# Half A's last mixer: from where its steps take their PSUM banks

## The chip, the core and the metric

The kernel runs on one core of one Trainium2 chip. The metric is the device time of one execution in microseconds, as the median of several runs. Shown beside it is one execution that the hardware profiler recorded, with its own time and the span from its first to its last instruction. The engines are TensorE (PE, matmuls and transposes; PEld is its loading of stationary operands), VectorE (DVE), ScalarE (ACT), GpSimd (POOL) and SyncE (SP), which issues most of the DMAs.

## The reference, cut to what matters

The program is one inference step of a two-layer encoder trunk over 1024 prompt frames and 64 frames of a running stream, width 1024, in fp32. Layer 0 mixes time with two linear recurrences, layer 1 with attention over bands of chunks. Each layer then has a SwiGLU channel mixer, and a layer norm follows each mixing:

```python
def swiglu(x, w_in, w_out):
    gate, up = jnp.split(x @ w_in, 2, axis=-1)
    return (jax.nn.silu(gate) * up) @ w_out
...
for layer in range(DEPTH):
    mix = ...   # layer 1: chunk_band_attention(x, ...), which ends with "@ w_o"
    x = layer_norm(DEEPNORM_ALPHA * x + mix, P['ln1_w'][layer], P['ln1_b'][layer])
    x = layer_norm(DEEPNORM_ALPHA * x + swiglu(x, P['ffn_w_in'][layer], P['ffn_w_out'][layer]),
                   P['ln2_w'][layer], P['ln2_b'][layer])
```

The attention has 16 heads of 64. A frame reads its own chunk of 64 frames and the 8 chunks before it, with a learned bias, a softmax, and the product with the values.

## The kernel before

**Halves.** The 1088 frames are worked on in two halves: half A (index 0) holds the first 384 prompt frames and the 64 stream frames, 448 columns; half B (index 1) holds the other 640 prompt frames. Each fp32 operand is split into a high and a low part (hi, lo), and a product is three matmuls: hi by hi, lo by hi, hi by lo. `gemm_ws` (lines 115 to 125, weights stationary) and `gemm_ts` (lines 127 to 137, frames stationary) issue them; their output tiles are all called gps. These are the dense products below.

**The mixer.** `ffn` (from line 915) is a generator that yields after each of 22 steps. A step loads two weight tiles of 512 KB (`load_w`, line 97 on SP, cast on line 100 on ACT, remainder on lines 105 on DVE and 107 on POOL), makes 2 x 24 matmuls of 448 columns for half A, and evacuates them on lines 927 to 940. After steps 3, 7, 11, 15, 17 and 21 the output group of `tsg` follows: its products with w_out go into the accumulators acc on lines 823 to 827. `load_w` has two raw buffers (wr) and four for each part (wh, wl); a mixer holds five hidden tiles (HB).

**The attention.** `attention(hf, hp, ...)` does two heads (a block, hp 0 to 7). It loads vt, ks, qs and bias on SP, then for each tile of 128 queries: scores (lines 1279 and 1280) into the PSUM tile sps, the sum with the bias and the maximum on DVE (1283), the exponential on ACT (1288), the division on POOL (1290), transposes into tp (1295), and the split into ph and pl (1305, 1306). For each group of tiles follow the products with the values (1321) into op and the evacuation, lines 1325 (ACT) and 1326 (DVE). A half-B block has four such groups, so its fourth line 1326 is its end. Its output goes to DRAM (og_d, line 1330, issued by ACT).

**PSUM.** There are eight banks. The pool gp has three from the start. The attention's pool atps has five: one sps of two banks and three of the tag t. When atps is closed, the pool gp2 may take these five. `bank()` gives out the tiles of the dense products, by a counter:

```python
self.bcount += 1
if self.gp2 and self.bcount % 8 > 2:
    return self.gp2.tile([128, 512], F32, tag="g2", name="gps", bufs=5)
return self.gp.tile([128, 512], F32, tag="g", name="gps", bufs=3)
```

Three numbers of eight fall to gp and five to gp2, once gp2 is there; the counter runs on either way.

**The order around the change.** Layer 1 of half B's attention is written as a loop over the blocks 2 to 7 with two steps of half A's last mixer behind each, steps 0 to 11 (blocks 0 and 1 come earlier, between half B's q and k products). Behind the loop the mixer's steps go on. At step `JM` = 16 the text turns to half B: it loads the attention's output from og_d into xh and xl (`load_xt`, lines 213 to 215, issued behind step 16's last weight load), loads the residual into acc, and runs `proj` with w_o (k-tiles 4 to 7 first, then 0 to 3), with the mixer's steps 17 to 20 between its tiles. xh and xl lie where ph and pl of the last blocks were. After that half B's last mixer, `s_ffn`, ends the kernel.

The text's order isn't the order on the engines. The framework makes every engine's queue when the program is built, going by the text's order and taking a later piece where an earlier one isn't ready; a tile of a pool that was opened in the place of another waits for the release of what lay there.

Of the kernel before, what the change touches and what calls it, by code (L numbers as in the profile page):

```python
# [14 lines left out]
PS = bass.MemoryType.PSUM  # L15
# [67 lines left out]
class Kern:  # L83
# [1249 lines left out]
    def run(self):  # L1333
        nc, tc, a = self.nc, self.tc, self.a
# [133 lines left out]
                for _ in range(2):  # L1468
                    next(f)
        es_at.close()  # L1470
        self.gp2 = self.ctx.enter_context(tc.tile_pool(name="gp2", bufs=1, space=PS))
        self.tpsum = self.bank
        for j in f:
            if j == self.JM:
                accp = self.ctx.enter_context(tc.tile_pool(name="accB1", bufs=1, side="right"))
                self.xt[1] = self.xt_tiles(xbp, 1)
                with tc.tile_pool(name="yr2", bufs=1, side="right") as yp, tc.issue_after(self.last_w):
                    self.load_xt(1, self.og_d, (4, 5, 6, 7, 0, 1, 2, 3), pool=yp)
                    self.paired = True
                    acc1 = self.load_acc(1, self.x_d, accp)  # L1480
                xs, sums = self.s_operands(self.ctx.enter_context(tc.tile_pool(name="sx", bufs=1, side="right")),
                                           self.ctx.enter_context(tc.tile_pool(name="st", bufs=1, side="right")))
                self.proj(1, acc1, "w_o", self.layer_norm(1, acc1, "ln1", 1, sums=sums), between=lambda i: next(f) if i < 4 else None)
# [89 lines left out]
```

## Time and profile before

| | us |
|---|---|
| median of 3 runs | 3156.28 (3156.26 to 3160.05) |
| profiled execution | 3154.14 |
| its span, first to last instruction | 3152.4 |
| PE busy in it | 3036.0 |
| DVE, ACT, POOL busy | 2019.7, 1263.5, 1353.0 |
| DRAM moved by DMA | 395.10 MB |

Rows of the profile read as follows. A row of a table by stretches has the start and end of the stretch, its length, and for each engine the busy us with the count of instructions; then the mean clock that PE was granted (1.00 is full), the share of the DMA engines, and GB/s. A row in order of time has the start, the us, the engine, the line of the kernel, the operation, output <- input by the program's names, their size, the count of merged instructions, and in brackets the idle time before it and what ended that. SPq and ACTq are DMA issues on the queues of SP and ACT. Matmuls are pipelined, so the spacing of their starts, not the length of one, is what each costs.

### The profile page before, as it was taken

The numbers are of one execution on the slowest core, as the hardware profiler recorded it, in microseconds if no ns is written. First come the engines' busy times: TensorE is split into PE (matmuls) and PEld (weight loads), VectorE is DVE, ScalarE is ACT, GpSimd is POOL, SyncE is SP. The second block draws the span as 40 slices with busy tenths as digits, with TensorE's granted clock in tenths as the row PEclk, the third lists the DMA queues.
The fourth block names the chain that finished last, engine by engine and source line by source line (L and its number), as shares of the span: only waits on it lengthen the run. The fifth ranks groups of instructions, "written<-read, shape, count | busy, mean of one in ns | idle before, by whom it ended". The sixth has DMA issues, their size and how long they took to land.

```text
span 3152.4 us, 50043 instructions
## 1 busy us (share of the span) xinstructions
PE 3036.0 (96%) x17468; PEld 2695.1 (85%) x17468; DVE 2019.7 (64%) x4933; ACT 1263.5 (40%) x2753; POOL 1353.0 (43%) x1481
## 2 busy tenths in 40 slices
PE   8999998899999999999999999999998899899998
PEld 7888887788888878888899898999996788799987
DVE  5677885979898664465553645355565458866567
ACT  4454553335445324244342223354444323333332
POOL 2354433545454234343332323344454335754444
PEclk9989999789999999999999999999998899999999
DMA  6553444434434238434433224765454143322122
GB/s 204 139 158 112 111 123 112 145 99 121 134 104 111 87 127 281 138 115 121 117 114 98 82 92 155 227 185 163 139 147 117 63 150 98 113 94 94 62 86 74
DMA packets 297340, 395.10 MB, mean 125 GB/s; under 512 B 125376, under 2 KB 218424, under 8 KB 297088
## 3 DMA queue, kind: packets, MB, share of 16 engines
q1 hardware_dynamic: 295936, 389.28, 41.5%
q8 instruction: 138, 2.26, 0.3%
q10 hardware_dynamic: 1152, 2.62, 0.2%
q14 instruction: 114, 0.93, 0.1%
HBM read 319.44 MB, written 75.51 MB: 125 GB/s over the span
## 4 chain that ended last, share of the span: by engine, by line
PE 79%; DVE 9%; DMA 5%; POOL 3%; issue 3%; ACT 2%; SPq 0%; POOLq 0%; DVEq 0%; ACTq 0%
PE gps L123 11%; PE gps L124 11%; PE gps L125 11%; PE gps L134 8%; PE gps L135 7%; PE gps L137 7%; PE gps L1058 2%; PE gps L1059 2%; PE gps L1060 2%; PE op L1321 2%; PE tp L1295 2%; DVE t L548 1%; PE sps L1279 1%; DVE x L550 1%; PE ps L621 1%
## 5 line engine op out<-in xcount | busy, mean ns | idle before, releaser
L107 POOL TENSOR_TENSOR wl<-wr,wh 128x512 fp32r<-128x512 f32 (+2 forms) x289 | 509.3, 1766 | 680.7 <-ACT wh L100 634.2
L123 PE MATMUL gps<-xh,wh 128*128 128x320 f32 (+1 forms) x2188 | 749.6, 343 | 8.7 <-ACT xh L214 6.1
L124 PE MATMUL gps<-xl,wh 128*128 128x320 f32 (+1 forms) x2188 | 747.7, 342 | 0.6 <-DVE xl L215 0.6
L125 PE MATMUL gps<-xh,wl 128*128 128x320 f32 (+1 forms) x2188 | 745.1, 341 | 0.8 <-DVE wl L105 0.7
L100 ACT CAST wh<-wr 128x1024 fp32r<-128x1024 f32 x352 | 367.4, 1048 | 503.8 <-PE gps L124 166.4
L105 DVE TENSOR_TENSOR wl<-wr,wh 128x512 fp32r<-128x512 f32 (+2 forms) x289 | 286.0, 990 | 264.0 <-ACT wh L100 261.8
L123 PEld LDWEIGHTS gps<-xh,wh 128*128 128x128 f32 x2188 | 416.7, 191 | 30.5 <-ACT xh L214 6.1
L125 PEld LDWEIGHTS gps<-xh,wl 128*128 128x128 f32 x2188 | 415.9, 190 | 19.2 <-DVE wl L105 1.5
L124 PEld LDWEIGHTS gps<-xl,wh 128*128 128x128 f32 x2188 | 416.2, 190 | 18.4 <-DVE xl L215 1.0
L1290 POOL TENSOR_SCALAR s<-s,mx 128x640 f32<-128x640 f32 (+5 forms) x144 | 203.0, 1410 | 268.2 <-DVE mx L1289 234.5
L134 PE MATMUL gps<-wh,xh 128*128 128x512 f32 x661 | 261.5, 400 | 3.2 <-ACT xh L1088 2.5
L137 PE MATMUL gps<-wh,xl 128*128 128x512 f32 x661 | 259.1, 398 | 4.8 <-DVE xl L215 4.8
L135 PE MATMUL gps<-wl,xh 128*128 128x512 f32 x661 | 261.8, 398 | 0.9 <-DVE wl L105 0.9
L135 PE MATMUL gps<-wl,hh 128*128 128x512 f32 x572 | 226.4, 397 | 0.0
L134 PE MATMUL gps<-wh,hh 128*128 128x512 f32 x572 | 226.0, 398 | 0.3 <-DVE acc L825 0.3
L825 DVE TENSOR_TENSOR acc<-acc,gps 128x512 f32<-128x512 f32 x216 | 143.4, 678 | 92.0 <-PE gps L137 87.5
L137 PE MATMUL gps<-wh,hl 128*128 128x512 f32 x484 | 189.9, 398 | 2.6 <-DVE hl L938 2.6
L548 DVE TENSOR_TENSOR t<-lt,x 16x48 f32<-16x48 f32 (+9 forms) x540 | 156.7, 290 | 39.9 <-DMA lt<-l_d 29.5
L1288 ACT ACTIVATE s<-s,mx 128x640 f32<-128x640 f32 (+5 forms) x144 | 96.4, 670 | 164.1 <-DVE mx L1287 160.9
L134 PEld LDWEIGHTS gps<-wh,xh 128*128 128x128 f32 x661 | 125.4, 190 | 32.6 <-ACT xh L1088 2.9
L137 PEld LDWEIGHTS gps<-wh,xl 128*128 128x128 f32 x661 | 124.9, 189 | 32.3 <-DVE xl L215 5.3
L135 PEld LDWEIGHTS gps<-wl,xh 128*128 128x128 f32 x661 | 125.5, 190 | 28.9 <-DVE wl L105 1.9
(355 smaller groups left out, 6353.6 us busy)
## 6 DMA issues: line engine op xcount, KB each, us to landing
wr<-in_w_fi SPq DMA_DIRECT2D x176, 512.0 KB
wr<-in_w_fo SPq DMA_DIRECT2D x88, 512.0 KB
wr<-in_w_in SPq DMA_DIRECT2D x44, 512.0 KB
wr<-in_w_qk SPq DMA_DIRECT2D x32, 512.0 KB
qs<-qd SPq DMA_DIRECT2D x32, 320.0 KB
wr<-in_w_om SPq DMA_DIRECT2D x16, 512.0 KB
wr<-in_w_v SPq DMA_DIRECT2D x16, 512.0 KB
vd<-vh SPq DMA_DIRECT2D x16, 512.0 KB
```

Of the source, the lines that this page charges most:

```text
L100: self.A.copy(hi, raw)
L105: self.V.tensor_tensor(lo[:, :h], raw[:, :h], hi[:, :h].bitcast(F32), op=ALU.subtract)
L107: self.G.tensor_tensor(lo[:, h:], raw[:, h:], hi[:, h:].bitcast(F32), op=ALU.subtract)
L123: self.T.matmul(ps, hi[:, kt, :], xh, start=(kt == 0), stop=False)
L124: self.T.matmul(ps, hi[:, kt, :], xl, start=False, stop=False)
L125: self.T.matmul(ps, lo[:, kt, :], xh, start=False, stop=(kt == nk - 1))
L134: self.T.matmul(ps, xh, wh, start=(i == 0), stop=False)
L135: self.T.matmul(ps, xh, wl, start=False, stop=(lo is None and i == n - 1))
L137: self.T.matmul(ps, cols(lo(kt)), wh, start=False, stop=(i == n - 1))
L548: V.tensor_tensor(tv, lt[:, j, w:16].unsqueeze(2).to_broadcast([m, r, w]), x[:, 0, j, 0:w].unsqueeze(1).to_broadcast([m, r, w]), op=ALU.mult)
L825: self.V.tensor_tensor(a, a, ps[:m], op=ALU.add)
L1290: G.tensor_scalar(s[:m, :nk], s[:m, :nk], mx[:m, 3:4], None, op0=ALU.mult)
```

## The change

The opening of gp2, and the line that has transposes take their PSUM tiles from `bank()`, move from right behind the attention loop into the body for step 16. Between the loop and that point gp2 is unset, and `bank()` answers with tiles of gp alone.

```diff
         es_at.close()
-        self.gp2 = self.ctx.enter_context(tc.tile_pool(name="gp2", bufs=1, space=PS))
-        self.tpsum = self.bank
         for j in f:
             if j == self.JM:
+                self.gp2 = self.ctx.enter_context(tc.tile_pool(name="gp2", bufs=1, space=PS))
+                self.tpsum = self.bank
                 accp = self.ctx.enter_context(tc.tile_pool(name="accB1", bufs=1, side="right"))
                 self.xt[1] = self.xt_tiles(xbp, 1)
```

The body for step 16 runs after that step has been written out, so steps 12 to 16 and the output group behind step 15 are what it concerns. They make no transposes.

## The prediction

> **What bounds the kernel now.** I read the page first, then the busy time by stretches around the edited lines, then each engine's rows there in order of time.
>
> ```profile
> PE 3036.0 (96%) x17468; PEld 2695.1 (85%) x17468; DVE 2019.7 (64%) x4933; ACT 1263.5 (40%) x2753; POOL 1353.0 (43%) x1481
> PE 79%; DVE 9%; DMA 5%; POOL 3%; issue 3%; ACT 2%; SPq 0%; POOLq 0%; DVEq 0%; ACTq 0%
> ```
>
> TensorE (PE) is the bound of the whole: 96% busy and 79% of the chain that ended last. An edit that only moves work pays where PE is idle or slow. So the next view is the table of stretches around the end of half B's attention.
>
> ```profile
> core 0: us, PE busy (x) PEld busy (x) DVE busy (x) ACT busy (x) POOL busy (x), PEclk, DMA share, GB/s
> 2314.00:2395.00 81.00, 79.88 (x447) 72.44 (x445) 50.65 (x120) 39.34 (x76) 41.75 (x32) 1.00 0.45 128
> 2395.00:2484.90 89.90, 65.16 (x298) 53.54 (x298) 44.57 (x139) 38.76 (x92) 42.44 (x32) 0.72 0.33 87
> 2484.90:2555.80 70.90, 70.88 (x328) 63.54 (x329) 32.44 (x44) 23.04 (x30) 28.65 (x17) 0.97 0.47 167
> 2555.80:2600.60 44.80, 44.80 (x193) 36.09 (x193) 19.73 (x28) 7.84 (x8) 13.01 (x8) 1.00 0.23 73
> ```
>
> The second stretch is the weak one: 24.7 us of PE idle, and a granted clock of 0.72 for what did run. The same table for the tile gps alone (the dense products) says why:
>
> ```profile
> 2397.00:2484.90 87.90, 0.00 (x0) 0.00 (x0) 0.00 (x0) 0.00 (x0) 0.72 0.32 83
> 2526.10:2546.10 20.00, 20.00 (x89) 16.55 (x89) 5.91 (x9) 0.00 (x0) 1.00 0.86 325
> 2546.10:2555.80 9.70, 9.70 (x49) 8.99 (x48) 1.99 (x3) 0.54 (x1) 1.00 0.52 178
> ```
>
> Not one dense matmul runs from 2397 to 2484.9 while the last attention blocks finish alone. Steps 12 to 15 of half A's mixer follow up to 2526.1, their output group takes 20.0 us, step 16 takes 9.7 us. PE's and SP's rows show what step 12 waited for:
>
> ```profile
> 2483.59 0.41 PE L1321 MATMUL op<-xl,vt 128*128 128x128 f32 x1
> 2484.92 0.74 PE L123 MATMUL gps<-xh,wh 128*128 128x448 f32 x1 [0.91 <-DVE o L1326]
> ...
> 2367.94 14.76 SPq L97 DMA_DIRECT2D wr<-in_w_fi  x3
> ...
> 2397.19 0.85 SPq L97 DMA_DIRECT2D wr<-in_w_fi  x2
> ```
>
> Its weights had been on their way since about 2368 (those of step 14 went out at 2397), so it was not data. What released it is line 1326, the last read of an attention bank. The counter in bank() agrees: the calls before step 12 are 92 (input projections), 108 (half A, layer 0), 24 (vproj and qk), 168 (half B's projection and mixer), 16 (w_o), 42 (vproj and qk) and 48 (steps 0 to 11), 498 in all. The next is 499, 3 modulo 8, so gp2: step 12 asks for banks that the attention still holds.
>
> **The change part by part.** It adds and removes no instruction. Until step 16 is issued gp2 is unset, so the 18 banks of steps 12 to 16 (two a step, eight for the group) come from the three of gp, which the attention never holds. The wait at 2484.92 goes, and these steps may slip in among the attention's matmuls, as steps 0 to 11 did. How those shared PE with the attention gives the price. First the ends of the attention blocks hp 2 to 7 (every fourth row of line 1326), then the ends of the output groups of steps 0 to 3, 4 to 7, 8 to 11, and two successive steps:
>
> ```profile
> 2220.68 0.42 DVE L1326 TENSOR_TENSOR o<-op,ot 64x256 f32<-64x256 f32 x1
> 2287.52 0.42 DVE L1326 TENSOR_TENSOR o<-op,ot 64x256 f32<-64x256 f32 x1
> 2353.98 0.42 DVE L1326 TENSOR_TENSOR o<-op,ot 64x256 f32<-64x256 f32 x1
> 2407.47 0.42 DVE L1326 TENSOR_TENSOR o<-op,ot 64x256 f32<-64x256 f32 x1 [0.57 <-ACT ot L1325]
> 2448.34 0.42 DVE L1326 TENSOR_TENSOR o<-op,ot 64x256 f32<-64x256 f32 x1 [0.34 <-ACT ot L1325]
> 2484.45 0.42 DVE L1326 TENSOR_TENSOR o<-op,ot 64x256 f32<-64x256 f32 x1 [2.90 <-ACT ot L1325]
> ...
> 2233.11 0.69 DVE L827 TENSOR_TENSOR acc<-acc,gps 64x512 f32<-64x512 f32 x1
> 2313.51 0.69 DVE L827 TENSOR_TENSOR acc<-acc,gps 64x512 f32<-64x512 f32 x1
> 2394.36 0.69 DVE L827 TENSOR_TENSOR acc<-acc,gps 64x512 f32<-64x512 f32 x1
> ...
> 2337.25 0.62 DVE L932 SCALAR_TENSOR_TENSOR ht<-ht,gps 128x448 f32<-128x448 f32 x1 [1.21 <-PE gps L125]
> 2350.68 0.62 DVE L932 SCALAR_TENSOR_TENSOR ht<-ht,gps 128x448 f32<-128x448 f32 x1 [1.03 <-PE gps L125]
> ```
>
> With dense work between, a block takes 66.5 us (2287.52 to 2353.98) and four steps with their group 81 us (2313.5 to 2394.4), with PE full. Alone, the last block takes 36.1 us (2448.34 to 2484.45). The dense steps run ahead of their place: at 2395 all twelve are through, and the attention is only (2395 - 2354) / 66.5 = 0.62 into hp 5, with 2.38 blocks to go.
>
> Carry that pace on. Steps 12 to 15 with their group last 81 us more and step 16 about 13.4 us (the two successive steps above), up to 2489.4. In these 94.4 us the attention does 94.4 / 66.5 = 1.42 blocks, which leaves 0.96, alone again, at 36.1 us each: 34.8 us. The attention then ends at 2524.2, 39.7 us later than now, but with all five steps behind it.
>
> **The cover that goes.** In the kernel before, steps 12 to 16 also hid the way of the last attention block to half B's w_o projection: store to DRAM, load, split. Now nothing is left to hide it, since steps 17 and on are queued behind w_o's weights and first products. Its rows:
>
> ```profile
> 2484.90 0.33 ACTq L1330 DMA_DIRECT2D og_d<-o  x1
> GB/s 0 0 0 0 0 0 0 0 128 410 371 410 307 13 0 0 0 0 0 0 0 0 0 0 0 0 0 0 0 0 0 0 0 0 0 0 0 0 0 0
> ...
> 2529.51 3.78 SPq L213 DMA_DIRECT2D yraw<-og_d  x8
> 2533.61 1.59 ACT L214 CAST xh<-yraw 128x640 fp32r<-128x640 f32 x2 [5.92 <-DMA yraw<-og_d]
> 2539.71 2.15 POOL L215 TENSOR_TENSOR xl<-yraw,xh 128x640 fp32r<-128x640 f32 x1
> 2548.94 3.51 POOL L107 TENSOR_TENSOR wl<-wr,wh 128x512 fp32r<-128x512 f32 x2 [1.88 <-ACT wh L100]
> ```
>
> (The GB/s row is the stretch 2484 to 2492 in slices of 0.2 us.) The chain is: 0.4 us for line 1326, 1.9 us for the store (issued at 2484.90, last packets at 2486.8), 4.1 us for a load (2529.51 to 2533.61; at best the 1.9 us of the store, of the same size), 0.8 us for the cast, 2.2 us for the subtraction on POOL: 7 to 9.5 us. PE may use 2 us of it for k-tiles 4 to 6, which need only older blocks (nine matmuls of the group row's 20.00 / 88 = 0.23 us). I take 7 us of idle PE. The lower bound is 1.5 us, a cast and a subtraction, if other banks' k-tiles 4 to 6 fill in. The upper bound is 25 us: all loads wait for the attention's SBUF, and w_o's weights stand behind them in SP's queue, as now (2529.51 to the end of the weights' subtraction at 2552.5 is 23 us, plus the 1.9 us store). I stay near the low end because SP will have idle weight buffers from 2489 on, so w_o's first weights can go out before the loads that wait.
>
> After such a gap the clock starts low:
>
> ```profile
> 2488.82 0.57 PE L124 MATMUL gps<-xl,wh 128*128 128x448 f32 x1
> 2489.20 0.57 PE L125 MATMUL gps<-xh,wl 128*128 128x448 f32 x1
> ...
> 2494.11 0.36 PE L124 MATMUL gps<-xl,wh 128*128 128x448 f32 x1
> 2494.31 0.37 PE L125 MATMUL gps<-xh,wl 128*128 128x448 f32 x1
> ```
>
> Starts 0.38 us apart against 0.20 once warm, from 2484.9 to about 2489.6: 12 matmuls with 0.17 us lost on each, 2 us. That comes back ahead of w_o.
>
> **Sum.** The w_o projection begins at 2524.2 + 7 + 2 = 2533.2 in effect, against 2555.8: 22.6 us earlier. From there on the work is that of before. What moves with the matmuls: on SP the weight loads of steps 14 to 16 and of the group pass the attention's last loads of ks, qs, bias and vt; on ACT, DVE and POOL their casts and subtractions and the steps' own evacuations come among the softmax pieces. In the stretch 2314 to 2395 the steps and the attention shared all these queues in the same way, with DVE at 50.65 of 81 us and the others lower, so this is priced in the 66.5 us. The one wait that the change sets anew, that of the w_o products for the attention's banks, falls away as they need the attention's output in any case. The profiled execution took 3154.1 us (span 3152.4), 2.1 under the median of 3156.3; taken off the median: **3134 us**.
>
> **Rivals.**
>
> *The attention keeps up.* Should the steps last until the attention ends, the 24.7 us of idle time and the slow clock both go. Work left at 2395 at full clock: 4 x 9.7 + 20.0 + 9.7 = 68.5 us dense. Attention needs 81 - 58.8 = 22.2 us of PE per 81 us, 18.2 us a block, 43.4 us for 2.38. PE would be through at 2507 instead of 2555.8, and with 9 us for the gap and restart 40 us are won: 3116. Against it: in 160 us the steps ran ahead steadily.
>
> *Three banks are too few.* If every bank's evacuation were exposed (an estimate of 1.2 us: the DVE rows of 0.62 and 0.69, and as much again for ACT's pass ahead of them), 18 banks cost 22 us and nothing is won: 3156. Against it, dense work on three banks alone, long before the edited lines, in half B's first mixer, and three banks beside the attention:
>
> ```profile
> 1700.00:1760.00 60.00, 60.00 (x344) 55.02 (x344) 21.22 (x30) 11.84 (x15) 12.56 (x9) 1.00 0.23 71
> 2260.00:2290.00 30.00, 30.00 (x170) 27.70 (x169) 19.14 (x46) 14.89 (x28) 16.56 (x13) 1.00 0.49 135
> ```
>
> No idle PE in either. The Trainium skill, "Perfetto Trace Analysis", section Matmul Optimizations, wants all 8 PSUM banks in use. By that rule the five steps would lose, which these two rows speak against.
>
> *The order stays.* The diff only lifts a dependency; the order of PE's queue is made at build time. If the steps still come last, or the gain is eaten by the 25 us way above (2524.2 + 25 + 2 = 2551, 5 us won), the time is 3151 to 3157.
>
> *Slower: the attention starves.* The order puts dense matmuls wherever the attention isn't ready, and each on PE's in-order queue holds the next attention step up. If during the 94.4 us the attention does x blocks instead of 1.42, it ends at 2489.4 + 36.1 (2.38 - x). With 9 us behind it, that passes 2555.8 once x is below 0.80. At x = 0.4 the projection begins 14 us late: 3170. For it: the pace did fall from 36.1 to 66.5 us a block. Against it: it was steady at that.
>
> **How the numbers follow.** About 0.2% (6.3 us) can be told from no change here. Forecast 0.62; attention keeps up 0.10; three banks 0.05; order stays 0.10; starving 0.13. Faster: 0.62 less 0.02 for a forecast that shrinks, 0.10, and 0.02 of the order case, 0.72. Slower 0.13, within 0.15. The range takes in the idle way from 1.5 us (28 us won) to 25, most of the first rival's surplus (37 won), and the no-gain cases: 3119 to 3156. Left out are the slower case and the far end of the first rival.
>
> **What would show it.** Right: gps matmuls between 2397 and 2484; step 16 done near 2489; the last line 1326 near 2524, later than now; then one gap of 5 to 10 us on PE before line 134 on xh, with a low clock at its start. A last line 1326 at 2510 or earlier speaks for the first rival, beyond 2545 for the slower one; many idle pieces of about 1 us before line 123 for the banks; an unchanged empty stretch for the order. A gap above 20 us with w_o weights landing last would make my 7 us wrong. A change downstream of w_o that I do not foresee would break the sum.

## The result and the profile after

The changed kernel takes 3127.44 us (median of 4 runs, 3125.41 to 3128.28), the kernel before 3158.16 us beside it: ratio 0.990, 95% interval 0.9883 to 0.9917. Forecast were 3134 us in a range of 3119 to 3156. The profiled execution took 3125.41 us with a span of 3123.6, 28.8 us under that of before, where the prediction's sum had 22.6.

PE does the same 17468 matmuls and is busy for 96% of the span as before, but 25.3 us less of it (3010.7 against 3036.0). So only 3.5 of the 28.8 us are idle time of PE; the rest is time in which PE counted as busy, in a stretch that had a mean clock of 0.72 before. The last block, still alone, and the gap behind it keep much of the idle time. From the page:

```profile
PE 3010.7 (96%) x17468; PEld 2674.1 (86%) x17468; DVE 2016.3 (65%) x4933; ACT 1263.9 (40%) x2753; POOL 1350.6 (43%) x1481
```

The dense products by stretches (the table for the tile gps; it was empty from 2397 to 2484.9), and then two rows of the table for all tiles:

```profile
2395.00:2430.00 35.00, 27.32 (x125) 23.23 (x126) 2.90 (x6) 1.63 (x3) 1.00 0.65 180
2430.00:2460.00 30.00, 23.58 (x102) 18.34 (x101) 5.10 (x8) 0.54 (x1) 1.00 0.36 99
2460.00:2490.00 30.00, 21.37 (x92) 16.81 (x92) 5.32 (x8) 0.54 (x1) 1.00 0.61 178
2490.00:2520.00 30.00, 0.00 (x0) 0.00 (x0) 0.00 (x0) 0.00 (x0) 0.87 0.07 27
...
2490.00:2520.00 30.00, 18.02 (x99) 14.98 (x99) 14.70 (x47) 13.01 (x31) 12.86 (x7) 0.87 0.07 27
2520.00:2540.00 20.00, 15.41 (x57) 12.37 (x58) 6.45 (x7) 5.76 (x8) 6.70 (x4) 0.77 0.72 266
```

Dense work now fills the attention up to about 2487 at full clock. What is left of the weak stretch is some 30 us of the last block, alone, and then a gap. In order of time (ends of output groups, ends of blocks 5 to 7, step 16's end, the gap):

```profile
2394.65 0.69 DVE L827 TENSOR_TENSOR acc<-acc,gps 64x512 f32<-64x512 f32 x1
2415.90 0.42 DVE L1326 TENSOR_TENSOR o<-op,ot 64x256 f32<-64x256 f32 x1 [1.01 <-ACT ot L1325]
2475.04 0.69 DVE L827 TENSOR_TENSOR acc<-acc,gps 64x512 f32<-64x512 f32 x1
2482.32 0.42 DVE L1326 TENSOR_TENSOR o<-op,ot 64x256 f32<-64x256 f32 x1 [0.57 <-ACT ot L1325]
2486.52 0.36 PE L125 MATMUL gps<-xh,wl 128*128 128x448 f32 x1
2518.04 0.42 DVE L1326 TENSOR_TENSOR o<-op,ot 64x256 f32<-64x256 f32 x1 [2.66 <-ACT ot L1325]
2524.59 0.79 PE L134 MATMUL gps<-wh,xh 128*128 128x512 f32 x1 [6.99 <-ACT xh L214]
```

The attention ends 33.6 us later than before, with five steps behind it. The w_o products begin at 2524.6 instead of 2555.8. From there to the end it is 599.0 us (3123.6 - 2524.6) against 596.6, the 2.4 us being mostly the slow clock behind the gap. The rest is the same work at the same pace; one stretch of it, 31 us apart, of after and then of before:

```profile
2570.00:2620.00 50.00, 49.41 (x245) 43.62 (x244) 37.44 (x66) 16.71 (x30) 24.48 (x22) 1.00 0.31 95
```
```profile
2601.00:2651.00 50.00, 49.41 (x245) 43.63 (x245) 38.09 (x65) 17.77 (x32) 24.16 (x22) 1.00 0.29 94
```

The gap read in the changed kernel's rows, and in the waits of SP's queue:

```profile
2463.82 13.28 SPq L97 DMA_DIRECT2D wr<-in_w_o  x4
...
2483.05 7.03 SPq L97 DMA_DIRECT2D wr<-in_w_o  x2
2520.76 3.65 SPq L213 DMA_DIRECT2D yraw<-og_d  x8
...
2518.49 0.33 ACTq L1330 DMA_DIRECT2D og_d<-o  x1
2523.81 1.49 ACT L214 CAST xh<-yraw 128x640 fp32r<-128x640 f32 x2 [5.80 <-DMA yraw<-og_d]
...
SPq L213 <- DMA og_d<-o: 30.5, 1, 30.5
```

Six of the eight w_o weight tiles went out ahead, from 2463.8 on. All eight loads of the attention's output waited for the store of the last block, those of older blocks too: SP stood 30.5 us at the first.

### The profile page after: what moved, and what is told of

Its sections match the earlier page's. It is cut to its first block, busy times and chain, and to the rows that moved or that the text cites. A ratio compares the mean times of both kernels' runs of the same rounds, so it can differ in the third digit from the quotient of the medians.

```text
span 3123.6 us, 50022 instructions
## 1 busy us (share of the span) xinstructions
PE 3010.7 (96%) x17468; PEld 2674.1 (86%) x17468; DVE 2016.3 (65%) x4933; ACT 1263.9 (40%) x2753; POOL 1350.6 (43%) x1481
## 3 DMA queue, kind: packets, MB, share of 16 engines
q1 hardware_dynamic: 295936, 389.28, 41.8%
## 4 chain that ended last, share of the span: by engine, by line
PE 79%; DVE 8%; DMA 5%; issue 3%; POOL 3%; ACT 2%; SPq 1%; POOLq 0%; DVEq 0%; ACTq 0%
PE gps L123 11%; PE gps L124 11%; PE gps L125 11%; PE gps L134 8%; PE gps L135 7%; PE gps L137 7%; PE gps L1058 3%; PE gps L1059 2%; PE gps L1060 2%; PE op L1321 2%; PE tp L1295 2%; DVE t L548 1%; DVE x L550 1%; PE sps L1279 1%; PE sps L1280 1%
## 5 line engine op out<-in xcount | busy, mean ns | idle before, releaser
L107 POOL TENSOR_TENSOR wl<-wr,wh 128x512 fp32r<-128x512 f32 (+2 forms) x289 | 502.9, 1744 | 634.8 <-ACT wh L100 583.9
```

The lines of the kernel that those rows point to most:

```text
L107: self.G.tensor_tensor(lo[:, h:], raw[:, h:], hi[:, h:].bitcast(F32), op=ALU.subtract)
```

## The experiments

Each ratio is to runs of the kernel before made beside it. All these kernels do the same work ahead of the edited place, yet their profiled executions reach it up to 15 us apart (T0 below). Profiles are therefore compared from one point, T0: the last line 827 of the output group of steps 8 to 11 (2394.4 before, 2394.7 after). "Filled" is the dense work that ran before the attention's end, at the full-clock prices of the prediction (9.7 us a step, 20.0 the group of four, about 10 the group of two).

| kernel | filled us | T0 | attention's end - T0 | w_o start - T0 | end - T0 | ratio to before, 95% interval |
|---|---|---|---|---|---|---|
| before | 0 | 2394.4 | 90.1 | 161.5 | 758.0 | |
| the change | 68.5 | 2394.7 | 123.4 | 129.9 | 728.9 | 0.990 (0.9883 to 0.9917) |
| a2_after_again | 68.5 | 2395.4 | 122.7 | 129.1 | 729.4 | 0.9926 (0.9910 to 0.9942) |
| e1_order_kept | 0 | 2407.2 | 89.7 | 159.7 | 757.8 | 1.0001 (0.9989 to 1.0012) |
| e2_gp2_at_13 | 34 | 2402.7 | 99.1 | 134.3 | 730.5 | 0.9916 (0.9901 to 0.9931) |
| e3_gp2_at_15 | 59 | 2397.2 | 124.0 | 136.4 | 732.9 | 0.9924 (0.9911 to 0.9937) |
| e5_gp2_16_body_17 | 70 | 2404.2 | 124.5 | 151.7 | 729.3 | 0.9909 (0.9896 to 0.9922) |
| e4_jm17 | 88 | 2400.4 | 134.9 | 141.3 | 721.7 | 0.9901 (0.9883 to 0.9919) |
| e5b_jm18 | 98 | 2392.3 | 140.8 | 147.3 | 726.2 | 0.9913 (0.9893 to 0.9933) |
| e6_early_loads | 68.5 | 2397.6 | 129.4 | 127.1 | 726.0 | 0.9899 (0.9882 to 0.9916) |
| e7_jm17_early | 88 | 2394.6 | 136.8 | 135.2 | 716.2 | 0.9863 (0.9844 to 0.9882) |
| e8_jm17_early_spread | 88 | 2395.6 | 136.8 | 135.2 | 718.0 | 0.9889 (0.9869 to 0.9908) |

(In the three kernels with early loads, e6, e7 and e8, the last line 1326 stands behind other DVE work, so the w_o products begin before it.)

**Three banks, order kept.**

```diff
-                        T.matmul(oo, wv, pp, start=(x + l == 0), stop=(x + l == len(order)))
+                        self.last_at = T.matmul(oo, wv, pp, start=(x + l == 0), stop=(x + l == len(order))).ins
...
-        for j in f:
+        with tc.issue_after(self.last_at):
+            for _ in range(self.JM - 12):
+                next(f)
+            j = next(f)
+        for j in [j]:
             if j == self.JM:
...
```

> Steps 12 to 16 keep the three banks of the change, but all their TensorE instructions are queued behind the attention's last matmul, as in the kernel before. Fill theory (the gain is dense work in the attention's idle and slow TensorE time, three banks cost nothing): the gain is gone, ratio to the kernel before 1.000 within 0.002, with no dense matmul between 2397 and 2484, and steps 12 to 16 with their group in 71 us as before. Bank rival (three banks expose the evacuations): ratio 1.004 to 1.007 (up to 22 us slower), with repeated idle pieces of about 1 us ahead of line 123. Wait rival (the gain comes from the lifted wait on the banks itself, the order being secondary): the ratio stays at 0.990.

Measured: 757.8 us from T0 against 758.0, ratio 1.0001. Its table for gps is empty where that of before was:

```profile
2430.00:2460.00 30.00, 0.00 (x0) 0.00 (x0) 0.00 (x0) 0.00 (x0) 0.71 0.33 70
2460.00:2490.00 30.00, 0.00 (x0) 0.00 (x0) 0.00 (x0) 0.00 (x0) 0.81 0.14 46
```

The whole gain is the order. The three banks cost nothing: behind the attention the steps take 41.0 us, their group 20.1, step 16 9.9, against 41.2, 20.0 and 9.7 with eight. The bank and wait rivals fall.

**gp2 at step 13.**

```diff
         for j in f:
-            if j == self.JM:
+            if j == 13:
                 self.gp2 = self.ctx.enter_context(tc.tile_pool(name="gp2", bufs=1, space=PS))
                 self.tpsum = self.bank
+            if j == self.JM:
```

> The opening of gp2 moves to step 13, so only steps 12 and 13 can go among the attention; steps 14 to 16 wait for its banks. Fill theory: two steps fill 26.8 us, the attention does 0.40 block in it instead of 0.71, and ends near 2496; steps 14 to 16 and the group follow in 51 us and hide the way of the last block, so the w_o products begin near 2548 without a gap: 7 to 11 us gained of the change's 29 to 31, ratio 0.9965 to 0.9975. Wait rival: all or nothing, ratio 0.990 or 1.000.

Measured: 27.5 us won from T0, far more than 7 to 11. The edit moved more than I meant. Step 14's first bank is the counter's 503, 7 modulo 8, on gp2; its second and both of step 15 are 0, 1 and 2, on gp. So seven of the eight banks of steps 12 to 15 went among the attention, 168 matmuls (eight of them ahead of T0), 34 us; one bank and the group were left. The gps rows, then the attention's end and the one bank behind it:

```profile
2402.70:2447.70 45.00, 35.02 (x160) 29.17 (x158) 3.14 (x5) 1.07 (x2) 1.00 0.64 180
2447.70:2501.50 53.80, 0.00 (x0) 0.00 (x0) 0.00 (x0) 0.00 (x0) 0.90 0.23 63
...
2501.85 0.42 DVE L1326 TENSOR_TENSOR o<-op,ot 64x256 f32<-64x256 f32 x1 [1.78 <-ACT ot L1325]
2502.32 0.47 PE L123 MATMUL gps<-xh,wh 128*128 128x448 f32 x1 [0.91 <-DVE o L1326]
```

These 34 us delayed the attention by only 9.0. The group and the rest, still behind it, hid the last block's way, so no gap opened. It neither proves nor breaks the fill theory, but it shows that half of the fill brings nearly all of the gain.

**gp2 at step 15** (the same edit with 15).

> gp2 opens at step 15: steps 12 to 15 and their group fill, step 16 waits for the attention's banks and lies between the attention and the w_o products. Fill theory with the way of the last block as the price that is left: the attention ends 4 to 8 us sooner than with the change (2510 to 2514), step 16's 9.7 us and 2 us of low clock hide the 7 us gap, and the w_o products begin near 2525 at full clock: the same time as the change within 3 us, ratio to the kernel before 0.989 to 0.991. If the gap were no cost of its own (TensorE work in all being what counts), it would lose the fill of step 16, about 5 us, against the change.

Measured: 732.9 from T0, 3.5 to 4.0 us behind the change's two profiles, a little outside the 3 us that I allowed. Attention's end, step 16 behind it, and the w_o products:

```profile
2521.22 0.42 DVE L1326 TENSOR_TENSOR o<-op,ot 64x256 f32<-64x256 f32 x1 [2.51 <-ACT ot L1325]
2521.70 0.74 PE L123 MATMUL gps<-xh,wh 128*128 128x448 f32 x1 [0.91 <-DVE o L1326]
...
2533.59 0.39 PE L134 MATMUL gps<-wh,xh 128*128 128x512 f32 x1
```

The gap is gone and the clock is back at the w_o products (596.5 us from there), as expected. But the attention ended no sooner for step 16 being out of its way, 124.0 instead of 123.4; I had expected 4 to 8. Taken alone that says that step 16 rides free in the change, and that this is worth more than the gap that it could hide. But the clock differs too. The last block, quite alone in both, took 37.9 us here and 33.9 with gp2 at 13; its stretch in the two, here first:

```profile
2483.40:2521.20 37.80, 25.83 (x120) 20.77 (x118) 17.78 (x54) 16.02 (x38) 15.57 (x9) 0.73 0.11 37
```
```profile
2468.00:2501.80 33.80, 24.40 (x122) 19.50 (x122) 17.69 (x54) 15.87 (x38) 16.52 (x9) 0.85 0.13 42
```

The clock was 0.73 against 0.85, and 4 us is the lower end of what I had expected. Whether step 16 costs the attention nothing is therefore not shown.

**w_o body at step 17, gp2 at 16.** The tiles of the w_o products come in the order 2, 0, 3, 1, 4; a step now goes behind each of the first three, instead of the first four.

```diff
-        self.HB, self.PRE, self.JO, self.JM = 5, 4, 16, 16
+        self.HB, self.PRE, self.JO, self.JM = 5, 4, 16, 17
...
-            if j == self.JM:
+            if j == 16:
                 self.gp2 = self.ctx.enter_context(tc.tile_pool(name="gp2", bufs=1, space=PS))
                 self.tpsum = self.bank
+            if j == self.JM:
...
-between=lambda i: next(f) if i < 4 else None)
+between=lambda i: next(f) if i in (2, 0, 3) else None)
```

> gp2 opens at step 16 as in the change, but the body with half B's w_o products comes one step later, at step 17 (three steps instead of four then go between its tiles). Step 17 and its group of two, some 20 us, need gp2 and so run right behind the attention, where they hide the way of the last block. Fill theory: attention end as with the change (2518), no 7 us gap, the w_o products at full clock: 6 to 9 us faster than the change, ratio 0.987 to 0.988, unless the one step fewer between half B's layer norms brings idle time there, up to 10 us. If the gap is hidden and the total still stays at the change's, the loss must show as idle TensorE time in the 100 us behind the w_o products.

Measured: 729.3 from T0, the same as the change; a miss. PE's idle pieces behind the attention:

```profile
2529.19 0.74 PE L123 MATMUL gps<-xh,wh 128*128 128x448 f32 x1 [0.91 <-DVE o L1326]
2543.61 0.50 PE L134 MATMUL gps<-wh,hh 128*128 128x512 f32 x1 [0.58 <-DVE ht L928]
2547.51 0.80 PE L134 MATMUL gps<-wh,hh 128*128 128x512 f32 x1 [2.93 <-DVE ht L932]
```

The 7 us gap is hidden, and gives way to the group's waits for step 17's hidden tile, which has no other step to cover it (0.58 and 2.93 us), at a clock that is low again (a mean of 0.80 over the two). Step 17 and its group took 26.7 us (125.0 to 151.7) instead of 19.7. Behind the w_o products nothing was lost: 577.6 us, 21.4 fewer than after the change.

**Both at step 17** (line for gp2 as in the change, the two other edits above).

> Both the opening of gp2 and the body with half B's w_o products move one step on, to step 17, so step 17 and its output group of two (19.7 us at full clock) may go among the last attention block too; three steps instead of four then go between the tiles of the w_o products. Fill theory with the marginal rate that the opening at step 13 against the change shows (30 us more of dense work let the attention end 24.3 us later): the attention ends 16 us later, the 7 us gap stays, 4 to 5 us gained on the change, ratio to the kernel before 0.988 to 0.990. If the last block runs at its own pace whatever is filled in, its idle 10 us and slow 2 us are won as well: 12 to 18 us, ratio 0.984 to 0.987.

Measured: 721.7 from T0, 7.2 to 7.7 us faster than the change's two profiles, ratio 0.9901 beside 0.9926 for the change on the same chip. It lies between my two estimates: 19.7 us more fill delayed the attention by 11.5 to 12.2.

```profile
2535.31 0.42 DVE L1326 TENSOR_TENSOR o<-op,ot 64x256 f32<-64x256 f32 x1 [1.78 <-ACT ot L1325]
2541.70 0.79 PE L134 MATMUL gps<-wh,xh 128*128 128x512 f32 x1 [6.83 <-ACT xh L214]
...
PE gps L896 <- POOL acc L889: 9.2, 1, 9.2
```

The gap stays (6.83), and the wait for half B's layer norm (line 889), 1.3 us in the change, is 9.2, where a fourth step used to lie.

**Both at step 18** (JM 18, steps between for the tiles 2 and 0 alone).

> The same two steps on, to step 18: steps 17 and 18 and the group, 29.5 us, may go among the last block, and two steps are left to go between the tiles of the w_o products and half B's layer norms. The last block has about 12 us of idle and slow TensorE time left in the change, so no more than that can be won there, and 2 to 9 us should be. Against it stands the cover between the layer norms: if two steps suffice, 2 to 9 us faster than the change; if not, idle time of 10 to 20 us shows in the 100 us behind the first w_o products and the result is slower than the change.

Measured: 726.2 from T0, 2.7 to 3.2 us under the change but 4.5 behind the opening at step 17. The attention ends 5.9 us later still and the waits for the layer norm's line 889 grow to 13.9 us. What the fill wins in front is given back as lost cover behind.

**Early loads.**

```diff
+                early = self.ap.tile([128, 2, D], F32, tag="gb", name="gb", bufs=1).rearrange("p j d -> p (j d)")
+                with tc.issue_after(self.last_w):
+                    for i, kt in enumerate((4, 5, 6)):
+                        raw = early[:, NB * i : NB * i + NB]
+                        nc.sync.dma_start(raw, self.og_d[kt])
+                        self.A.copy(self.xt[1].h(kt), raw)
+                        self.V.tensor_tensor(self.xt[1].l(kt), raw, self.xt[1].h(kt).bitcast(F32), op=ALU.subtract)
...
-                    self.load_xt(1, self.og_d, (4, 5, 6, 7, 0, 1, 2, 3), pool=yp)
+                    self.load_xt(1, self.og_d, (7, 0, 1, 2, 3), pool=yp)
```

> The change, with the output of blocks 4, 5 and 6 loaded ahead of the attention's end into the layer norm's constant buffer, idle there, instead of into SBUF that the attention holds until the store of its last block has landed. If the gap of 7 us ahead of the w_o products is that wait (SBUF and the store, then all eight loads at once), it falls to 1.5 to 3 us, TensorE begins with k-tiles 4 to 6, and 4 to 6 us are won, with the clock's 2 us in part: ratio to the kernel before 0.988 to 0.989. If the gap is k-tile 7's own way (store, load, cast, subtraction), it only moves behind the first matmuls: the w_o products begin sooner, stall after 2 us, and nothing is won.

Measured: the gap falls from 6.99 to 0.60 us, and no stall follows on k-tile 7:

```profile
2524.62 0.79 PE L134 MATMUL gps<-wh,xh 128*128 128x512 f32 x1 [0.60 <-ACT xh L1482]
```

So the gap was the wait for the attention's SBUF and the loads behind it, not k-tile 7's own way. Only 2.9 to 3.4 us were won, since the last attention matmul came 4 us later than in the change's profiles (126.1 against 122.5 and 121.8 from T0), at a lower clock (0.73 over the stretch in which the attention was alone, against 0.91); see the last section.

**Both, and the steps spread otherwise.** The edits of e4_jm17 and e6_early_loads together, and the same with `i in (0, 3, 1)`.

> Step 17 among the last attention block (the opening of gp2 and the w_o body at step 17) together with the early loads of blocks 4 to 6. From the end of the output group of steps 8 to 11 to the end the change takes 729.2 us, the first alone 721.7, the second alone 726.0. If the two gains lie on different idle time (the last block's, and the gap behind it), they add: 718 to 719 us, ratio to the kernel before 0.987 to 0.989, with the 9.2 us wait ahead of one transpose in half B's layer norm still there. If the early loads only shift the wait, 721 to 722.

> The same, with the three steps left placed behind the second, third and fourth tile of the w_o products instead of the first three. If the 9.2 us wait for half B's layer norm is the one tile that has no step beside it, it goes or shrinks, and 3 to 8 us are won on the sister kernel: 711 to 716 us from the same point. If the layer norm's own chain on DVE and POOL sets the pace there, the wait moves ahead of another transpose and the time stays within 2 us.

Measured: 716.2 us from T0, 12.7 to 13.2 us under the change, 41.8 under the kernel before; 3113.73 us median against 3156.21, ratio 0.9863 (0.9844 to 0.9882). The two gains add (7.5 and 3.2 make 10.7) and a little more. This beats both kernels. The gap, and the wait that is left:

```profile
2529.77 0.68 PE L134 MATMUL gps<-wh,xh 128*128 128x512 f32 x1 [0.70 <-ACT xh L1482]
...
PE gps L896 <- POOL acc L889: 9.2, 1, 9.2
```

Spreading the three steps cuts that wait, but 718.0 is no better. The wait for line 1028's casts, 0.9 us in e7_jm17_early, is 5.6 here; it was 5.7 in the change and 5.6 in e4_jm17 too, so its absence may be the little more that e7_jm17_early won:

```profile
PE gps L1058 <- ACT wh L1028: 5.6, 4, 2.7
PE gps L896 <- DVE acc L891: 4.5, 1, 4.5
```

**The change again.**

> The changed kernel itself, on the chip and beside the runs of the three others: 728.9 us within 1 us from the end of the output group of steps 8 to 11 to the end, the attention's last line 1326 at 123.4 behind that point, w_o products at 129.9; ratio to the kernel before 0.990 within 0.002.

Measured: 729.4 from T0, attention's end at 122.7, w_o at 129.1: the profile repeats within 1 us. Its ratio, 0.9926 (0.9910 to 0.9942), lies just outside the 0.002 that I allowed, and its interval overlaps the first. By medians the gain is 22.6 us here (3154.53 to 3131.92) and was 30.7 the first time: medians place it to some 8 us only, and what is finer in this document rests on the rows from T0, one or two profiles for each kernel.

## Why the prediction was right, and where it was off

- *The gain is dense work in the attention's idle and slow time.* Shown: the rows above, and with the order taken back the gain is gone (1.0001). The slow time counted for more than the idle time, of which PE lost only 3.5 us in all.
- *Three banks suffice.* Shown by the same run. The rule of the Trainium skill, "Perfetto Trace Analysis", section Matmul Optimizations, that all eight banks be in use, made no difference here: the same steps took the same time on three.
- *The pace of the shared stretch carries on.* Right: block 6 took 66.4 us (2415.90 to 2482.32) for 66.5, steps 12 to 15 and their group 80.4 for 81, the last block 35.7 for 36.1.
- *The position at 2395.* This term was mis-sized. "Only 0.62 into hp 5" spread a block's progress evenly over its 66.5 us, which puts its end at 2420.3; it ended at 2415.9. The groups of a block are uneven. Counted from the last finished group, as in block 4, it would have come out at 2417. With step 16 done at 2486.9 instead of 2489.4, the attention ended at 2518.0 and not 2524.2. That 6.2 us is the whole of the difference between 22.6 and 28.8.
- *The cover that goes.* 7 us forecast, 6.99 measured; 2 us for the clock, 2.4 measured from w_o to the end. The size was right, but part of its reason was not: I had k-tile 7's chain down as its core. The early loads show that it was the wait of all loads for the closed pool's memory, which I had as the upper case only; w_o's weights, which made that case 25 us, did go out ahead. That the two numbers agree to 0.01 us is luck: the forecast counted 2.2 us for the subtraction, which the first products did not wait for, and took off 2 us for k-tiles 4 to 6, which were not there in time.
- *The attention starves, or keeps up.* Neither: while the steps ran, up to 92.2 us behind T0, it finished blocks 5 and 6 and some 4.5 us of block 7, at the pace above, and 31 us of the last block were left alone. But the price of the fill is uneven: 34 us of it delayed the attention by 9.0 us (gp2 at 13), the last bank and the group, 25 us, by another 24.9 (gp2 at 15), step 16 by nothing that shows, step 17 and its group by about 12.

Why the group's fill is so dear is not settled. The attention ran alone at a mean clock of 0.90 from 2447.7 to 2501.5 with gp2 at 13, at 0.91 in the change (2487 to 2518) and at 0.74 with gp2 at 15 (2477 to 2521.7). So the clock enters these prices, and they are not prices of the fill alone; the order of the pieces may be the rest.

## What to carry to other kernels

When a stretch of one engine is empty, look for what the work behind it waits for: if it is the memory of a pool that was handed on, not data, a smaller share that is free may do as well, and one run with the order forced back tells the order's gain from the resource's cost. Work that is moved forward leaves something uncovered where it was; price that first, then see whether its wait is data or again memory that is handed on late. Where two streams interleave, read progress from the last finished piece, and compare profiles from a point right ahead of the edit.

## What was not expected of the hardware

The granted clock fell without any long idle piece. Three stretches of attention alone on PE: the last block's in the change and with the early loads, and one of the kernel before (busy time of PE and the other engines, then the granted clock, third from the end):

```profile
2495.00:2503.00 8.00, 5.25 (x37) 4.69 (x38) 5.20 (x17) 4.13 (x11) 4.26 (x3) 1.00 0.00 0
```
```profile
2498.00:2506.00 8.00, 6.99 (x29) 6.13 (x29) 3.27 (x12) 3.16 (x9) 4.11 (x3) 0.57 0.00 0
```
```profile
2420.00:2440.00 20.00, 14.97 (x59) 12.22 (x59) 9.66 (x30) 8.49 (x20) 9.81 (x8) 0.59 0.14 32
```

The same kind of work got 1.00 in one profile and 0.57 in another, and 0.59 in a stretch of the kernel before whose longest idle piece was about 1 us. The Trainium skill, "TensorE: Matmul & The Clock Gate", Part 1, has the clock fall after an idle window of some 3.4 us; here a PE that was idle for an eighth (6.99 of 8 us busy) to a quarter (14.97 of 20) of the time, in pieces of 1.7 us at most, lost it as well, and not each time. A stretch like that costs more than its idle time, by an amount that differs between kernels whose queues there are nearly the same (4 us between the change and the early loads). What decides it is not shown.
